# Hymba encoder layer on one core: the head projections of group A for two pairs of heads at a time, v and z_a with 512 weight columns a product

## The chip, the cores and the metric

One core of a Trainium2 chip runs the whole layer in one launch. The metric is the device time of an execution in microseconds. The kernel before took 1144.22 us (median of 3 runs, 1143.96 to 1146.23). Every array is float32 in memory; TensorE is fed with float32r, a shortened form of it.

## The reference, cut to what matters

The sequence has 256 tokens, the model 2048 channels, group A 16 heads of 128.

```python
hn   = rmsnorm(x, norm_w)
proj = hn @ w_in                       # 2048 x 18432: q, v, f_fwd, f_bwd, z_a, b, c, h, z_b
# group A, each head, both directions
f    = lb + (1 - lb) * sigmoid(f_logit);  k = 1 - f;  q = silu(q)
b    = cumsum(log f) in chunks of 64
o    = masked(q exp(b - b_mid) @ (k exp(b_mid - b)).T) @ v  +  (q exp(b)) @ state
o_a  = head_rmsnorm(o_fwd + o_bwd) * silu(z_a)
# group B
o_b  = rmsnorm(b * conv3(c * h)) * silu(z_b)
h    = x + concat(o_a, o_b) @ w_out
h    = h + (p @ w_ple) * sigmoid(h @ w_ple_gate)
out  = rmsnorm(h, final_norm_w)
```

## The kernel before

**Products in three parts.** A float32 operand is split into a high part that float32r holds exactly and a low part, the rest. ScalarE copies the high part (line 70), VectorE subtracts it (line 71). A product is then high x high + high x low + low x high, so each weight quarter of 1024 columns per partition costs one copy and one subtraction. `Stream` (lines 31 to 81) keeps a list of all weight blocks in the order of use, loads 1 MB at a time into three buffers (`raw`, on SyncE's queue) and splits quarters (`spl`, five buffers) three quarters ahead of their use. The activations `xs` are split once and stay.

**One block.** A block is 256 columns of `w_in` against all 2048 channels and 256 tokens, in 16 steps over the channels and two halves m. In each step and half there are two matmuls: one with 512 moving columns and one with 256 (lines 290 and 291). *Column-major* blocks (f_fwd, f_bwd, q and all of group B) hold the weights still and stream `xs` (high and low, 256 tokens each); *token-major* blocks (z_a and v) hold `xs` still and stream 256 weight columns, high and low. Each half of a block fills one PSUM buffer (`a`, four of them); `evac` adds its two halves with one ScalarE copy and one VectorE operation per m.

**Group A.** The loop runs over 8 pairs of heads. Each pair has the blocks f_fwd, f_bwd, q, z_a, v in this order, four weight quarters each. When z_a is done, `mix_pair` computes from f and q the forget gates, the cumulative sums (`tensor_tensor_scan` on VectorE), the exponentials, and on GpSimd the scaled copies kc, qc, kx. Two things then need TensorE for each head: `scores` (32-row products into `scps`, then the four `cx` products) and `outputs` (products of `s` and `sx` with `vt`). They are put among the blocks by `at(dt, fn)`: fn is issued when the counter of steps, which `tick()` raises once for each of the 16 steps of a block, is dt higher. For a pair the scores come 20 and 34 steps after `mix_pair`, the outputs 30 and 44; for the first pair all of them 16 steps later. `finish_pair`, called from the next pair's `mix_pair`, scales the outputs by their norm and sets `turn` 16 and 24 steps later: two transposes into the PSUM buffer `kv`, of which there is one, then ScalarE (line 368) and VectorE (line 369) write the two parts of `mixa`.

**The order on each engine** is made by a scheduler that places the recorded instructions by priority and dependence; the splits get a higher priority, so that they move ahead of the attention's work. On each engine instructions then run in the order that it left.

**First pair.** The first three blocks run together under a hand-written order while `x` and the weights arrive (lines 322 to 331). Their sums sit in the four `a` buffers and in `kv` and `tr`. The norms of the tokens (`rx`, `rbc`) follow from a second load of x.

Of the kernel before, what the change touches and what calls it, by code (L numbers as in the profile page):

```python
# [17 lines left out]
P = 128  # L18
D = 2048
T = 256  # L20
# [10 lines left out]
class Stream:  # L31
# [10 lines left out]
    def add(self, src):  # L42

        j = len(self.todo)
        _, k, n = src.shape
        self.todo.append((src, k, n))
        first = len(self.where)
        self.where += [(j, h) for h in range(k * n // 1024)]
        return list(range(first, len(self.where)))

    def load(self, j, k0=0, k1=None, pool=None):
        src, k, n = self.todo[j]
        if j not in self.raws:
            tag = f"raw{j}" if pool else "raw"
            self.raws[j] = (pool or self.rawp).tile([P, 2048], F32, tag=tag, name=f"raw{j}")
        dst = self.raws[j][:, : k * n].rearrange("p (k n) -> p k n", n=n)
        self.nc.sync.dma_start(dst[:, k0:k1], src[:, k0:k1])

    def open(self, i):
        j, h = self.where[i]  # L60
        n = self.todo[j][2]
        if j not in self.raws:
            self.load(j)
        half = self.raws[j][:, h * 1024 : (h + 1) * 1024].rearrange("p (k n) -> p k n", n=n)
        part = self.splp.tile([P, 2048], F32R, tag="spl", name=f"spl{i}")
        self.parts[i] = part.rearrange("p (k s n) -> p k s n", s=2, n=n)
        return half, self.parts[i]

    def split(self, r, v):
        self.nc.scalar.copy(out=v[:, :, 0, :], in_=r)  # L70
        self.nc.vector.tensor_tensor(out=v[:, :, 1, :], in0=r, in1=v[:, :, 0, :], op=ALU.subtract)  # L71
# [13 lines left out]
def tile_hymba_encoder(  # L85
# [193 lines left out]
    def gemm_part(acc, w, g, token_major, k0=0, k1=4):  # L279
        for k in range(k0, k1):  # L280
            kt = 4 * g + k
            for m in range(2):
                a = acc[m].rearrange("p a b -> p (a b)")
                if token_major:
                    lh, ll = xs[:, kt, 0, m * P : (m + 1) * P], xs[:, kt, 1, m * P : (m + 1) * P]
                    rf, rh = w[:, k, :, :].rearrange("p s n -> p (s n)"), w[:, k, 0, :]
                else:
                    lh, ll = w[:, k, 0, m * P : (m + 1) * P], w[:, k, 1, m * P : (m + 1) * P]
                    rf, rh = xs[:, kt, :, :].rearrange("p s n -> p (s n)"), xs[:, kt, 0, :]
                pe.matmul(a, lhsT=lh, rhs=rf, start=(kt == 0), stop=False)  # L290
                pe.matmul(a[:, :T], lhsT=ll, rhs=rh, start=False, stop=(kt == NKT - 1))  # L291
            tick()

    def gemm_in(c, i, token_major):
        acc = acc_in(c, i)
        for g in range(4):
            gemm_part(acc, ws.get(blocks[c, i][g]), g, token_major)
        return acc

    def evac(acc, dst, tmpp, token_major=False):  # L300

        for m in range(2):
            r = tmpp.tile([P, T], F32, tag="r", name="r", bufs=3)
            if token_major:
                act.activation(r, acc[m][:, 1, :], AF.Copy, scale=rx[:, m : m + 1])
                dve.scalar_tensor_tensor(
                    out=dst(m), in0=acc[m][:, 0, :], scalar=rx[:, m : m + 1], in1=r, op0=ALU.mult, op1=ALU.add
                )
            else:
                act.copy(out=r, in_=acc[m][:, 1, :])  # L310
                dve.tensor_tensor(out=dst(m), in0=acc[m][:, 0, :], in1=r, op=ALU.add)
# [10 lines left out]
    with tc.manual_schedule(engines={ENG.Activation, ENG.DVE, ENG.PE}):  # L322
        for g in range(4):
            parts = [ws.open(ids3[c][g]) for c in range(3)]
            for k0, k1 in PIECES[g]:
                for k in range(k0, k1):
                    x_split(4 * g + k)
                for half, v in parts:
                    ws.split(half[:, k0:k1], v[:, k0:k1])
                for c in range(3):  # L330
                    gemm_part(acc3[c], parts[c][1], g, False, k0, k1)
# [20 lines left out]
    def finish_pair(i, ogz, ss):  # L352

        rs = ap_.tile([P, 4], F32, tag="rs", name=f"rs{i}", bufs=2)
        act.activation(rs, ss, AF.Sqrt, bias=epst, scale=1.0 / P)
        dve.reciprocal(out=rs, in_=rs)
        for m in range(2):
            for h in range(2):
                dve.tensor_scalar(
                    ogz[:, m, h, :], ogz[:, m, h, :], rs[:, 2 * m + h : 2 * m + h + 1], None, op0=ALU.mult  # L360
                )

        def turn(h):
            hd = 2 * i + h
            tp = psm.tile([P, 512], F32, tag="kv", name=f"ogt{hd}")
            for m in range(2):
                pe.transpose(tp[:, m * P : (m + 1) * P], ogz[:, m, h, :], ident)
            act.activation(mixa[:, hd, 0, :], tp[:, :T], AF.Copy, scale=hgw[:, hd : hd + 1])
            dve.scalar_tensor_tensor(
                out=mixa[:, hd, 1, :], in0=tp[:, :T], scalar=hgw[:, hd : hd + 1],  # L370
                in1=mixa[:, hd, 0, :], op0=ALU.mult, op1=ALU.subtract,
            )

        for h in range(2):
            at(16 + 8 * h, lambda h=h: turn(h))

    last_pair = [None]

    def mix_pair(i, xf, qt, zt, vt):

# [4 lines left out]
        for n, t in (("q", qt), ("z", zt)):  # L385
            sg = ap_.tile([P, 2, T], F32, tag="sg", name=f"s{n}{i}")
            act.activation(sg, t, AF.Sigmoid)
            pool.tensor_tensor(out=t, in0=t, in1=sg, op=ALU.mult)
# [13 lines left out]
        if last_pair[0] is not None:  # L402
            last_pair[0]()
# [50 lines left out]
        ogz = ap_.tile([P, 2, 2, P], F32, tag="ogz", name=f"ogz{i}", bufs=2)  # L454
        ss = ap_.tile([P, 4], F32, tag="ss", name=f"ss{i}", bufs=2)
# [58 lines left out]
        def outputs(h):  # L514
            s, sx = st[h]
            o = psm.tile([P, 2, P], F32, tag="o", name=f"o{i}_{h}")
            hs = slice(h * P, (h + 1) * P)
# [4 lines left out]
            for m in range(2):  # L522
                act.activation(junk, o[:, m, :], AF.Square, accum_out=ss[:, 2 * m + h : 2 * m + h + 1])
            dve.tensor_tensor(out=ogz[:, :, h, :], in0=o, in1=zt[:, :, hs], op=ALU.mult)


        late = 16 if i == 0 else 0
        for h in range(2):
            at(late + 20 + 14 * h, lambda h=h: scores(h))
            at(late + 30 + 14 * h, lambda h=h: outputs(h))  # L530
        last_pair[0] = lambda: finish_pair(i, ogz, ss)

    for i in range(8):
        xf = ap_.tile([P, 2, 2, T], F32, tag="xf", name=f"xf{i}", bufs=2)
        evac(acc3[0] if i == 0 else gemm_in(B_FF, i, False), lambda m: xf[:, 0, m, :], ap_)
        evac(acc3[1] if i == 0 else gemm_in(B_FB, i, False), lambda m: xf[:, 1, m, :], ap_)
        qt = ap_.tile([P, 2, T], F32, tag="qt", name=f"qt{i}")
        evac(acc3[2] if i == 0 else gemm_in(B_Q, i, False), lambda m: qt[:, m, :], ap_)
        zt = ap_.tile([P, 2, T], F32, tag="zt", name=f"zt{i}")
        acc = gemm_in(B_ZA, i, True)  # L540
        if i == 0:
            xctx.close()
        evac(acc, lambda m: zt[:, m, :], ap_, True)
        vt = ap_.tile([P, 2, T], F32, tag="vt", name=f"vt{i}")
        mix_pair(i, xf, qt, zt, vt)
        evac(gemm_in(B_V, i, True), lambda m: vt[:, m, :], ap_, True)
# [10 lines left out]
    for i in range(8):  # L557
        cg = ctmp.tile([P, 2, T], F32, tag="cg", name=f"cg{i}", bufs=2)
        evac(gemm_in(B_CG, i, False), lambda m: cg[:, m, :], ctmp)
        hb = ctmp.tile([P, 2, T], F32, tag="hb", name=f"hb{i}", bufs=2)  # L560
        evac(gemm_in(B_HB, i, False), lambda m: hb[:, m, :], ctmp)
        if i == 0:
            last_pair[0]()
# [11 lines left out]
        evac(gemm_in(B_BG, i, False), lambda m: hb[:, m, :], ctmp)  # L575
        pool.tensor_tensor(out=cg, in0=cg, in1=hb, op=ALU.mult)
        y2 = ctmp.tile([P, 2, T], F32, tag="y2", name=f"y2_{i}")
        act.activation(y2, cg, AF.Square)
        pool.tensor_tensor(out=ysum, in0=ysum, in1=y2, op=ALU.add)
        evac(gemm_in(B_ZB, i, False), lambda m: hb[:, m, :], ctmp)  # L580
        by_norms(hb, rbc, 2)
        sz = ctmp.tile([P, 2, T], F32, tag="szb", name=f"szb{i}")
# [211 lines left out]
```

## Time and profile before

| | |
|---|---|
| runs | 1143.96, 1144.22, 1146.23 us |
| profiled execution | 1147.19 us, of it 1145.4 us from the first to the last instruction |
| mean granted clock of TensorE | 0.993 of full speed |
| TensorE, VectorE, ScalarE, GpSimd busy | 1129.6, 737.6, 644.5, 214.2 us |
| one pair of group A, from the third pair on | 60.54 us |
| weights and inputs read | 211.11 MB, 186 GB/s over the span |

A line of the profile names engine, line of the kernel before, operation, tiles and shape. TensorE's matmuls overlap each other, so the length of one is not its cost: the distance from one start to the next is. "Idle before" is the engine's own idle time, and what stands behind the arrow ended it. PEclk is the share of TensorE's clock that was granted in a stretch.

### The profile page before, as it was taken

To read this page: it belongs to the slowest core of one execution; us is meant where nothing else is said; L and a number is where in the kernel's file an instruction comes from. 1 tells how busy PE (TensorE), PEld (TensorE's weight loads), DVE (VectorE), ACT (ScalarE), POOL (GpSimd) and SP (SyncE) were. 2 spreads that over 40 slices of the span, in tenths; PEclk is the share of its full clock that TensorE was granted. 3 is DMA by queue.
4 is the path that set the end of the run, shared out by engine and by line. 5 is a ranking of instruction groups with operands and counts; after the bars stand their busy time and mean duration, and the time that the engine had idled before them with its cause. 6 is when DMAs were issued, how large, how long until landed. Compare 5 with 4: busy or idle time off the path is not lost.

```text
span 1145.4 us, 16984 instructions
## 1 busy us (share of the span) xinstructions
PE 1129.6 (99%) x6832; PEld 980.5 (86%) x6832; DVE 737.6 (64%) x957; ACT 644.5 (56%) x899; POOL 214.2 (19%) x167
## 2 busy tenths in 40 slices
PE   8999999999999999999999999999999999999997
PEld 7878888888888888888888888888888888888887
DVE  6785859585858686775566566556656555555664
ACT  6685767584858585765544444444545434434554
POOL 1032414140413223232121111211211000000011
PEclk9998999999999999999999999999999999999998
DMA  8753545455455545464555555555557555565542
GB/s 294 294 187 119 185 159 188 161 185 182 152 182 178 174 163 185 152 215 152 191 196 195 186 184 189 188 198 180 203 184 266 188 196 190 198 215 189 201 167 75
DMA packets 33487, 214.31 MB, mean 187 GB/s; under 512 B 3712, under 2 KB 5120, under 8 KB 9088
## 3 DMA queue, kind: packets, MB, share of 16 engines
q1 hardware_dynamic: 33264, 213.14, 54.1%
q8 instruction: 54, 0.88, 0.3%
q14 instruction: 25, 0.20, 0.1%
q10 hardware_dynamic: 144, 0.08, 0.0%
HBM read 211.11 MB, written 2.10 MB: 186 GB/s over the span
## 4 chain that ended last, share of the span: by engine, by line
PE 97%; DMA 1%; DVE 0%; POOL 0%; ACT 0%; SPq 0%; issue 0%; ACTq 0%; DVEq 0%
PE a L290 46%; PE a L291 23%; PE pg L640 3%; PE pg L639 3%; PE pg L641 3%; PE pa L639 3%; PE pa L641 3%; PE pb L641 3%; PE pb L639 3%; PE pa L640 3%; PE pb L640 3%; PE cx L509 1%; PE scps L467 1%; PE o L520 1%; PE o L519 1%; DMA xf<-in_xt_dram 1%
## 5 line engine op out<-in xcount | busy, mean ns | idle before, releaser
L71 DVE TENSOR_TENSOR spl<-raw,spl 128x1024 fp32r<-128x1024 f32 (+2 forms) x397 | 501.7, 1267 | 326.1 <-ACT spl L70 325.4
L290 PE MATMUL a<-xs,spl 128*128 128x512 f32 x1792 | 633.8, 398 | 2.8 <-DVE xs L237 1.8
L70 ACT CAST spl<-raw 128x1024 fp32r<-128x1024 f32 (+2 forms) x397 | 407.5, 1029 | 350.3 <-PE a L291 213.0
L291 PE MATMUL a<-xs,spl 128*128 128x256 f32 x1792 | 500.9, 280 | 0.2 <-DVE spl L71 0.2
L290 PEld LDWEIGHTS a<-xs,spl 128*128 128x128 f32 x1792 | 338.1, 189 | 79.7 <-ACT spl L70 2.2
L291 PEld LDWEIGHTS a<-xs,spl 128*128 128x128 f32 x1792 | 339.6, 190 | 0.8 <-DVE spl L71 0.5
L290 PE MATMUL a<-spl,xs 128*128 128x512 f32 x512 | 178.4, 392 | 0.0
L291 PE MATMUL a<-spl,xs 128*128 128x256 f32 x512 | 143.4, 280 | 0.0
L290 PEld LDWEIGHTS a<-spl,xs 128*128 128x128 f32 x512 | 95.8, 187 | 21.3
L291 PEld LDWEIGHTS a<-spl,xs 128*128 128x128 f32 x512 | 96.8, 189 | 0.0
L310 ACT COPY r<-a 128x256 f32<-128x256 f32 x112 | 40.9, 368 | 45.4 <-PE a L291 45.4
L698 POOL TENSOR_TENSOR hh<-hh,fw 128x512 f32<-128x512 f32 (+1 forms) x10 | 11.5, 1152 | 259.2 <-ACT gt L697 249.7
L639 PE MATMUL pg<-spl,ht 128*128 128x512 f32 (+1 forms) x160 | 55.6, 348 | 0.0
L641 PE MATMUL pg<-spl,ht 128*128 128x512 f32 (+1 forms) x160 | 55.5, 347 | 0.0
L640 PE MATMUL pg<-spl,ht 128*128 128x512 f32 (+1 forms) x160 | 55.5, 347 | 0.0
L639 PE MATMUL pa<-spl,mixa 128*128 128x512 f32 x128 | 50.4, 394 | 0.0
L641 PE MATMUL pa<-spl,mixa 128*128 128x512 f32 x128 | 49.9, 390 | 0.0
L640 PE MATMUL pa<-spl,mixa 128*128 128x512 f32 x128 | 49.9, 390 | 0.0
L639 PE MATMUL pb<-spl,mixb 128*128 128x512 f32 x128 | 49.8, 389 | 0.0
L640 PE MATMUL pb<-spl,mixb 128*128 128x512 f32 x128 | 49.8, 389 | 0.0
L641 PE MATMUL pb<-spl,mixb 128*128 128x512 f32 x128 | 49.8, 389 | 0.0
L505 POOL TENSOR_TENSOR s<-scm 128x256 f32<-128x256 f32 x16 | 18.0, 1123 | 102.3 <-DVE scm L503 102.3
(167 smaller groups left out, 1092.4 us busy)
## 6 DMA issues: line engine op xcount, KB each, us to landing
raw<-in_w_in_dram SPq DMA_DIRECT2D x138, 1024.0 KB, 5.0
raw<-in_w_out_dram SPq DMA_DIRECT2D x32, 1024.0 KB, 5.0
raw<-in_w_gate_dram SPq DMA_DIRECT2D x12, 1024.0 KB, 5.0
raw<-in_w_gate_end_dram SPq DMA_DIRECT2D x4, 1024.0 KB, 4.9
raw<-in_w_in_dram SPq DMA_DIRECT2D x6, 512.0 KB, 11.1
raw<-in_w_in_dram SPq DMA_DIRECT2D x9, 256.0 KB, 6.4
xf<-in_xtok_dram SPq DMA_DIRECT2D x2, 1024.0 KB, 12.6
hh<-in_xtok_dram SPq DMA_DIRECT2D x1, 2048.0 KB, 8.2
```

Source lines behind the costliest of these rows:

```text
L70: self.nc.scalar.copy(out=v[:, :, 0, :], in_=r)
L71: self.nc.vector.tensor_tensor(out=v[:, :, 1, :], in0=r, in1=v[:, :, 0, :], op=ALU.subtract)
L290: pe.matmul(a, lhsT=lh, rhs=rf, start=(kt == 0), stop=False)
L291: pe.matmul(a[:, :T], lhsT=ll, rhs=rh, start=False, stop=(kt == NKT - 1))
L310: act.copy(out=r, in_=acc[m][:, 1, :])
L467: pe.matmul(scps[s0 : s0 + Q, 2 * d + hf, t0 : t0 + w], lhsT=lhsT, rhs=rhs, start=True, stop=True)
L505: pool.tensor_tensor(out=s, in0=sm[:, 0:2, :], in1=sm[:, 2:4, :], op=ALU.add)
L509: pe.matmul(cx[:, d, :], lhsT=kx[:, d, h, :], rhs=qc[:, d, h, :], start=True, stop=True)
L639: pe.matmul(acc[m], lhsT=lh, rhs=w[:, k, 0, :], start=(kt == 0), stop=False)
L640: pe.matmul(acc[m], lhsT=lh, rhs=w[:, k, 1, :], start=False, stop=False)
L641: pe.matmul(acc[m], lhsT=ll, rhs=w[:, k, 0, :], start=False, stop=(kt == nk - 1))
L698: pool.tensor_tensor(out=h, in0=h, in1=fw[:, cs], op=ALU.mult)
```

## The change

Group A goes by two pairs of heads (i and i + 1, four times). For both pairs the three column-major blocks f_fwd, f_bwd, q run first, six in a row. Then v of both pairs runs as one product of 512 weight columns (`gemm_two`), then z_a of both in the same way. In `gemm_two` a step and half has three matmuls of 512 columns (high x high, high x low, low x high) in place of two times 512 + 256, and `tick()` is called for each half, 32 times a product. A weight load for it is two transfers of 512 KB, one from each pair's block, side by side in one `raw` buffer. Its sum is taken out of PSUM by one ScalarE operation per m, with no VectorE operation.

`mix_pair` is cut in two: `mix_forgets` (norms, sigmoids, logarithms, forget gates) right behind each pair's q, and the rest, for the first pair at once and for the second 16 steps into v. z_a's gate (`gate_two`) and the scaling by the norm (`finish_two`) follow when both pairs' outputs exist, while the next two pairs' blocks run; the gate is now multiplied in there and `outputs` only copies. Counted in steps from the end of the six blocks, the scores stand at 9, 15, 46 and 52, the outputs at 38, 42, 55 and 61; for the first two pairs the scores are 18 and 12 steps later and the second pair's outputs 12. The four turns of two pairs are issued 48, 50, 52 and 54 steps after the next two pairs' first q block. The scratch `r` has two buffers instead of three, and in group B `y2` and `szb` share one.

```diff
     def load(self, j, k0=0, k1=None, pool=None):
-        src, k, n = self.todo[j]
+        srcs, k, n = self.todo[j]
...
+        for b, src in enumerate(srcs):
+            self.nc.sync.dma_start(dst[:, b, k0:k1], src[:, k0:k1])
...
-    for i in range(8):
-        for c in (B_FF, B_FB, B_Q, B_ZA, B_V):
-            blocks[c, i] = sum((ws.add(w_in[c + i, h]) for h in range(2)), [])
+    for i in range(0, 8, 2):
+        for ii in (i, i + 1):
+            for c in (B_FF, B_FB, B_Q):
+                blocks[c, ii] = sum((ws.add(w_in[c + ii, h]) for h in range(2)), [])
+        for c in (B_V, B_ZA):
+            blocks[c, i] = sum(
+                (ws.add(*(w_in[c + i + b, q // 2, :, 4 * (q % 2) : 4 * (q % 2) + 4] for b in range(2))) for q in range(4)), []
+            )
...
+    def gemm_two(c, i, dst):
+        acc = [psg.tile([P, 512], F32, tag="g", name=f"a{c}_{i}_{m}") for m in range(2)]
+        for kt in range(NKT):
+            w = ws.get(blocks[c, i][kt // 2])
+            for m in range(2):
+                lh, ll = xs[:, kt, 0, m * P : (m + 1) * P], xs[:, kt, 1, m * P : (m + 1) * P]
+                pe.matmul(acc[m], lhsT=lh, rhs=w[:, kt % 2, 0, :], start=(kt == 0), stop=False)
+                pe.matmul(acc[m], lhsT=lh, rhs=w[:, kt % 2, 1, :], start=False, stop=False)
+                pe.matmul(acc[m], lhsT=ll, rhs=w[:, kt % 2, 0, :], start=False, stop=(kt == NKT - 1))
+                tick()
+        for m in range(2):
+            act.activation(dst[:, m, :], acc[m], AF.Copy, scale=rx[:, m : m + 1])
...
-            dve.tensor_tensor(out=ogz[:, :, h, :], in0=o, in1=zt[:, :, hs], op=ALU.mult)
+            dve.tensor_copy(ogz[:, :, h, :], o)
...
-        late = 16 if i == 0 else 0
-        for h in range(2):
-            at(late + 20 + 14 * h, lambda h=h: scores(h))
-            at(late + 30 + 14 * h, lambda h=h: outputs(h))
+        late = 18 if i == 0 else 0
+        at(late + 9, lambda: steps[0][0](0))
+        at(late + 15, lambda: steps[0][0](1))
+        at(late + 16, lambda: steps.append(mix_pair(i + 1, *forgets[1])))
+        late = 12 if i == 0 else 0
+        at(38, lambda: out(0, 0))
+        at(42, lambda: out(0, 1))
+        at(late + 46, lambda: steps[1][0](0))
+        at(late + 52, lambda: steps[1][0](1))
+        at(late + 55, lambda: out(1, 0))
+        at(late + 61, lambda: out(1, 1))
+        gemm_two(B_V, i, vt)
+        gemm_two(B_ZA, i, zt)
+        def rest():
+            gate_two(i, zt)
+            at(30 if i < 6 else 6, lambda: finish_two(i, ogs, ss, zt))
+            for hd in range(4):
+                at((48 if i < 6 else 20) + 2 * hd, lambda hd=hd: turn(2 * i + hd, ogs[hd // 2]))
+        last_two[0] = rest
```

The order changes at three places that matter below. The first is VectorE some 78 us into the program, around the end of the fourth to sixth block. Before, the two operations on `vt0` free the PSUM buffers of the first pair's v; they stand behind the split of quarter 27:

```order
L71 TENSOR_TENSOR spl27_856<-raw13_827,spl27_856 128x4x256
L430 TENSOR_TENSOR gx_153<-dd0_645,pf0_644 128x2x3
L431 TENSOR_TENSOR gx_153<-pf0_644,lf0_635 128x2x3
L306 SCALAR_TENSOR_TENSOR vt0_625<-a8_0_0_677,few_79,r_759 128x256
L432 TENSOR_TENSOR gx_153<-gx_153,dd0_645 128x2x3
L306 SCALAR_TENSOR_TENSOR vt0_625<-a8_0_1_678,few_79,r_762 128x256
L438 TENSOR_TENSOR pf0_644<-qt0_477,pf0_644 128x512
L311 TENSOR_TENSOR xf1_765<-a16_1_0_766,r_848 128x256
```

In the changed kernel the buffers that the next product waits for there are those of the second pair's f_bwd (`a24_1`), and their two operations on `xf1` stand ahead of the split of quarter 26:

```order
L451 TENSOR_TENSOR gx_153<-dd0_634,pf0_633 128x2x3
L452 TENSOR_TENSOR gx_153<-pf0_633,lf0_624 128x2x3
L328 TENSOR_TENSOR xf1_487<-a24_1_0_674,r_756 128x256
L453 TENSOR_TENSOR gx_153<-gx_153,dd0_634 128x2x3
L328 TENSOR_TENSOR xf1_487<-a24_1_1_675,r_759 128x256
L77 TENSOR_TENSOR spl26_827<-raw13_824,spl26_827 128x2x512
L458 TENSOR_TENSOR dd0_634<-xf0_467,dd0_634 128x512
L459 TENSOR_TENSOR pf0_633<-qt0_468,pf0_633 128x512 x2
```

So the operations that free the PSUM buffers stand two splits nearer to the start. The second place is VectorE at the first pair's outputs, where the copy into `ogz0` frees the single PSUM buffer `o` for the second head's output. Before:

```order
L503 COPY_PREDICATED scm0_149<-tri_143,scps_155 128x512
L71 TENSOR_TENSOR spl30_945<-raw15_943,spl30_945 128x4x256
L71 TENSOR_TENSOR spl31_982<-raw15_943,spl31_982 128x4x256
L524 TENSOR_TENSOR ogz0_675<-o0_0_956,zt0_484 128x2x128
L311 TENSOR_TENSOR xf1_765<-a24_1_0_854,r_973 128x256
```

In the changed kernel (pf1 and dd1 are the second pair's cumulative sums, from `mix_pair(i + 1)`):

```order
L432 SCALAR_TENSOR_TENSOR pf1_1071<-smask_140,lf1_858 128x256
L436 SCALAR_TENSOR_TENSOR pf1_1071<-lf1_858,smask_140 128x256
L442 TENSOR_TENSOR dd1_1072<-pf1_1071 128x256
L445 TENSOR_TENSOR dd1_1072<-pf1_1071 128x256
L442 TENSOR_TENSOR dd1_1072<-pf1_1071 128x256
L77 TENSOR_TENSOR spl37_1136<-raw18_1108,spl37_1136 128x2x512
L445 TENSOR_TENSOR dd1_1072<-pf1_1071 128x256
L451 TENSOR_TENSOR gx_153<-dd1_1072,pf1_1071 128x2x3
L452 TENSOR_TENSOR gx_153<-pf1_1071,lf1_858 128x2x3
L453 TENSOR_TENSOR gx_153<-gx_153,dd1_1072 128x2x3
L544 COPY ogz0_1120<-o0_0_1121 128x2x128
```

The copy out of `o` now stands behind the second pair's scans. The third place is ScalarE at the turns of a steady pair. Before, one turn is among splits and copies:

```order
L70 CAST spl65_2008<-raw32_1982 128x4x256
L511 COPY sx2_0_1980<-cx2_0_1977 128x256
L70 CAST spl66_2029<-raw33_2027 128x4x256
L368 ACTIVATE mixa_460<-ogt3_2003,vec_81 128x256
L70 CAST spl67_2065<-raw33_2027 128x4x256
```

In the changed kernel (the second to fourth of four turns):

```order
L375 ACT_TABLE_LOAD
L375 ACTIVATE sq3_1926<-qt3_1641 128x512
L417 ACTIVATE mixa_460<-ogt1_1949,vec_81 128x256
L76 CAST spl70_2034<-raw35_2031 128x2x512
L417 ACTIVATE mixa_460<-ogt2_1960,vec_81 128x256
L530 COPY sx2_0_2020<-cx2_0_2017 128x256
L417 ACTIVATE mixa_460<-ogt3_1977,vec_81 128x256
L76 CAST spl71_2108<-raw35_2031 128x2x512
```

The four turns now follow each other with one or two instructions between, among the second pair's forget gates. On TensorE 12 matmuls of 512 columns stand between the first turn and the second, 15 and half of the scores between the second and third, and the other half of the scores, `cx` and 4 matmuls between the third and fourth.

More of the change, by code (lines that the diff above doesn't have):

```diff
@@ L330, in tile_hymba_encoder @@
                 for c in range(3):
[L331 removed]
+                    gemm_part(acc3[c], parts[c][1], g, k0, k1)
     rctx.close()
@@ L350, in c64, with mix_forgets @@
         return t.rearrange("p h (c t) -> p h c t", t=CH)
[L352 to L357, printed above, removed]
-            for h in range(2):
[L359 to L379, printed above, removed]
+    def mix_forgets(i, xf, qt):
         by_norms(xf.rearrange("p a b t -> p (a b) t"), rbc, 4)
@@ L522, in outputs @@
             for m in range(2):
[L523 to L540 removed]
+                act.activation(junk, o[:, m, :], AF.Square, accum_out=ss[:, m, h : h + 1])
@@ L549, in tile_hymba_encoder @@
+        last_two[0] = rest
+    for i in range(0, 8, 2):
+        two_pairs(i)
+    last_two[0]()
     mixb = None
```

141 lines of the change are left out of this document (90 added, 51 removed).

## The prediction

> **What bounds the kernel now.** I read the page first, its busy times and the chain that ended last.
>
> ```profile
> span 1145.4 us, 16984 instructions
> PE 1129.6 (99%) x6832; PEld 980.5 (86%) x6832; DVE 737.6 (64%) x957; ACT 644.5 (56%) x899; POOL 214.2 (19%) x167
> PE 97%; DMA 1%; DVE 0%; POOL 0%; ACT 0%; SPq 0%; issue 0%; ACTq 0%; DVEq 0%
> ```
>
> TensorE sets the end: 97% of the chain is matmuls following each other. So only three things can pay: fewer or shorter matmuls, less waiting of TensorE, or a higher clock. Whatever VectorE and ScalarE save is worth nothing unless TensorE was waiting for it. Next I read the waits of TensorE alone, those after the start:
>
> ```profile
> PE scps L467 <- POOL qc L446: 1.7, 1, 1.7
> PE a L290 <- DVE gx L432: 0.9, 1, 0.9
> PE scps L467 <- POOL kc L446: 0.8, 1, 0.8
> PE cx L509 <- POOL kx L452: 0.8, 1, 0.8
> ```
>
> Each occurs once, so they belong to one place, 4.2 us together. The busy times by stretch show where (the columns are the stretch, its length, the five engines' busy time, PEclk, DMA share, GB/s):
>
> ```profile
> 78.00:90.00 12.00, 7.76 (x75) 6.24 (x74) 9.21 (x15) 6.17 (x11) 6.96 (x6) 0.92 0.42 138
> 90.00:103.00 13.00, 13.00 (x103) 11.24 (x103) 5.48 (x7) 5.33 (x12) 0.55 (x1) 0.82 0.33 120
> 138.35:198.89 60.54, 60.54 (x432) 53.34 (x436) 43.86 (x61) 40.96 (x61) 16.55 (x11) 1.00 0.51 171
> 259.43:319.97 60.54, 60.54 (x432) 53.33 (x436) 44.07 (x61) 40.98 (x61) 16.56 (x11) 1.00 0.51 175
> ...
> 79.00:80.00 1.00, 0.54 (x3) 0.53 (x4) 0.78 (x3) 0.99 (x2) 0.00 (x0) 1.00 0.68 90
> 88.00:89.00 1.00, 0.32 (x1) 0.32 (x2) 0.72 (x1) 0.00 (x0) 0.83 (x2) 0.50 0.84 164
> 94.00:95.00 1.00, 1.00 (x5) 0.90 (x4) 0.16 (x1) 0.00 (x0) 0.00 (x0) 0.60 0.00 0
> 95.00:96.00 1.00, 1.00 (x7) 0.87 (x7) 0.00 (x0) 0.00 (x0) 0.00 (x0) 1.00 0.00 0
> ```
>
> A steady pair is 60.54 us in which TensorE never rests, while VectorE has 44 and ScalarE 41 us of work: no stall is left to remove there. In the 12 us from 78 on TensorE works only 7.76. These are the first pair's scores, whose kc, qc and kx come from GpSimd too late. Behind the idle time comes a second loss: from 88 to about 95 us the clock is half.
>
> **Term 1, fewer matmuls.** What a matmul costs is the distance of starts. I take a column-major stretch of group B (13 pairs of 512 + 256) and the output projection, whose three 512-column products have the form of the new ones:
>
> ```profile
> 600.33 0.39 PE L290 MATMUL a<-xs,spl 128*128 128x512 f32 x1
> ...
> 604.83 0.40 PE L290 MATMUL a<-xs,spl 128*128 128x512 f32 x1
> ...
> 919.96 0.39 PE L639 MATMUL pa<-spl,mixa 128*128 128x512 f32 x1
> ...
> 925.40 0.39 PE L639 MATMUL pa<-spl,mixa 128*128 128x512 f32 x1
> ```
>
> 4.50 us / 13 = 0.3462 us for 768 columns; 5.44 / 24 = 0.2267 us for 512. The old form needs two pairs, 0.6923 us, for what three new matmuls do in 0.6800: 12.3 ns less. There are 32 of these in each product, two products and four passes, 256 in all: **3.15 us**. The columns are the same, 1536 on both sides, so all of it is a fixed cost of a matmul, of which there are 256 fewer. Sum by the two rows: fixed part f = 12.3 ns, for 768 columns = 2f + 768c and 512 = f + 512c.
>
> The Trainium skill, in "TensorE: Matmul & The Clock Gate", section "Wait — 56ns, not 53.3ns?", states a fixed cost of only about 2.5 ns per matmul at full clock. By it term 1 would be 0.64 us; the rows here show five times that, for this float32r form with a weight load ahead of every matmul, so I keep 3.15.
>
> **Term 2, the stall at the first pair.** The scores of pair 0 move from 36 steps behind `mix_pair` to 27 steps into v, behind two whole blocks: `mix` is issued in step 15 of f_fwd(1), the scores 48 + 27 − 15 = 60 steps later. The first 33 of these are column-major steps of 0.69 us, the last 27 take 0.68, so 41 us, where before 36 x 0.69 = 25 us missed by 3.3. The chain ahead has the same work plus the second pair's `by_norms` (one GpSimd operation and a sigmoid), so 1.7 + 0.8 + 0.8 = 3.3 us go.
>
> The 0.9 us have another cause, PSUM. The next block needs the buffers of v(0), which VectorE emptied late:
>
> ```profile
> 77.55 1.21 DVE L71 TENSOR_TENSOR spl<-raw,spl 128x1024 fp32r<-128x1024 f32 x1
> ...
> 78.84 0.47 DVE L306 SCALAR_TENSOR_TENSOR vt<-a,few,r 128x256 f32<-128x256 f32 x1
> ...
> 79.31 0.47 DVE L306 SCALAR_TENSOR_TENSOR vt<-a,few,r 128x256 f32<-128x256 f32 x1
> ...
> 79.46 0.47 PE L290 MATMUL a<-xs,spl 128*128 128x512 f32 x1 [0.90 <-DVE gx L432]
> ```
>
> The same buffer rule holds for the changed kernel (v(0) needs f_bwd(1)'s), but the order has two splits fewer ahead, 2 x 1.2 = 2.4 us, more than 0.9. So it goes too: **4.2 us** for both. If it does not, 0.9 come back.
>
> **Term 3, the clock.** PEclk 0.92 over 12 us and 0.82 over 13 are 0.96 + 2.34 = 3.3 us of clock; half of the 0.68 us in which TensorE was idle from 88 to 89 comes off: **2.9 us**. In the steady pairs, and from 79 to 80 in the middle of the lone 0.9 us wait, PEclk is 1.00, so single waits of that size do not cost clock.
>
> **Term 4, new waits.** The pieces, by groups of instructions:
>
> ```profile
> L71 DVE TENSOR_TENSOR spl<-raw,spl 128x1024 fp32r<-128x1024 f32 (+2 forms) x397 | 501.7, 1267 | 326.1 <-ACT spl L70 325.4
> L70 ACT CAST spl<-raw 128x1024 fp32r<-128x1024 f32 (+2 forms) x397 | 407.5, 1029 | 350.3 <-PE a L291 213.0 <-PE pb L641 53.1 <-PE pa L641 41.5
> L310 ACT COPY r<-a 128x256 f32<-128x256 f32 x112 | 40.9, 368 | 45.4 <-PE a L291 45.4
> L387 ACT ACT_TABLE_LOAD x15 | 19.2, 1283 | 12.3 <-DVE zt L306 12.1
> L411 DVE TENSOR_TENSOR_SCAN pf<-smask,lf 128x256 f32<-128x256 f32 x16 | 17.2, 1074 | 0.0
> L503 DVE COPY_PREDICATED scm<-tri,scps 128x512 f32<-128x512 uint32 x16 | 11.8, 739 | 2.3 <-PE scps L467 2.3
> L415 DVE TENSOR_TENSOR_SCAN pf<-lf,smask 128x256 f32<-128x256 f32 x16 | 10.8, 673 | 0.0
> L369 DVE SCALAR_TENSOR_TENSOR mixa<-ogt,vec,mixa 128x256 fp32r<-128x256 f32 x16 | 7.6, 475 | 0.0
> L368 ACT ACTIVATE mixa<-ogt,vec 128x256 fp32r<-128x256 f32 x16 | 7.5, 470 | 0.0
> L524 DVE TENSOR_TENSOR ogz<-o,zt 128x256 f32<-128x256 f32 x16 | 6.7, 421 | 6.7 <-ACT jk L523 6.7
> L421 DVE TENSOR_TENSOR dd<-pf 128x256 f32<-128x256 f32 x16 | 6.7, 419 | 0.3
> ```
>
> *The first pair's second output* (once). It needs the buffer `o`, freed by the copy into `ogz0`. Ahead of that on VectorE stand, from the end of the scores: the mask 0.74, four scans 2 x 1.07 + 2 x 0.67 = 3.49, four subtractions 1.68, one split 1.27, the copy 0.42, about 7.6, plus half of a split that is under way, 0.6: 8.2 us. TensorE has meanwhile 9 steps x 0.68 = 6.1, the `cx` products 0.64 and the first output, which I count like `cx`: 7.4. Wait 0.8; ends 0 and 2.1 (a whole split more). I take **0.7**. In later passes the scores are 23 steps ahead of the outputs and it is covered.
>
> ```profile
> 138.35 0.70 PE scps L467 x31
> 139.05 0.64 PE cx L509 x4
> ```
>
> *The turns* (three passes among v, a fourth in group B). `kv` is one buffer: the second turn waits until ScalarE and VectorE have read the first. Behind the first turn stand a copy of q's sum 0.37, a split's copy 1.03, on VectorE its subtraction 1.27, and line 369's 0.48: 3.15 us against 12 x 0.2267 = 2.72 on TensorE, 0.4 of waiting. The second turn has a table load 1.28, a sigmoid and a split ahead against 15 matmuls, 3.4 us, and some 0.15 of scores; the third mask and split against scores and `cx`, 0.7 + 0.64, and 4 matmuls, 0.9. Both come out near zero. The lower end is 0 (the scheduler placed the matmuls between for this), the upper one table load more, 0.4 + 1.28 = 1.7 per pass. I take 0.5, nearest to the one chain that I can add up: **1.5 us** for three, 0 to 5.1. Behind a waiting turn queue v's matmuls alone; their splits are three quarters ahead.
>
> **Edits at nothing.** Per two pairs VectorE loses eight operations of line 306 and ScalarE gets 4 longer ones for 8; the gates only move. Both stay under the 44 and 41 of 60.5 us above, so TensorE covers them, and if it did not they would show as waits for `spl`. The 64 transfers of 512 KB replace 32:
>
> ```profile
> raw<-in_w_in_dram SPq DMA_DIRECT2D x138, 1024.0 KB, 5.0
> ```
>
> 1 MB lands in 5.0 us and is used up in two quarters per 2.7 us, three buffers deep; SyncE's queue carries nothing else then. An issue more per MB, even if its landing took half as long again, stays hidden behind the two buffers ahead.
>
> **Sum.** 3.15 + 4.2 + 2.9 − 0.7 − 1.5 = 8.05 us. On the profiled execution's own 1147.19 us (1145.4 and 1.8 around it) this is 1139.1. The median shown is 2.97 lower, just about term 3: these runs may have kept the clock. If so, 1144.22 − 5.15 = 1139.1; if not, 1136.2. I say **1138**.
>
> **Rivals.**
> - *Turns become the bound, slower.* If a table load, a split's copy and its subtraction stand ahead of each later turn (1.28 + 1.03 + 1.27, with the turn's own 0.47 + 0.48 in all 4.5 us against 2.7), each waits 1.8, a pass 5.4, and as at 88 us the clock drops for 2.9 more. Three passes of 8.3 less the 10.25 gained: 1144.2 + 25 − 10 = 1159; the waits decide from 10.25 / 3 = 3.4 us per pass on. For it: ScalarE's order. Against: 0.4 for the only chain that I can close. 10%.
> - *The first stall stays.* v(0) waits for f_bwd(1)'s buffers and the scores for GpSimd after all, since VectorE worked 9.2 of the 12 us from 78 on. Terms 2 and 3 fall out: 1144.2 − 3.15 + 2.2 = 1143.3. Against: 16 us more slack. 12%.
> - *No new wait.* 1144.2 − 10.25 = 1134. 18%.
> - *Term 1 is not there*: with `xs` held still and splits read through two strides, three products take the 0.6923 us of the old two pairs; 1138 + 3.15 = 1141.2. Against: the output projection's rows. 4%. By the skill's 2.5 ns a matmul, above, it would be 1140.5.
>
> **Chances.** Forecast 56%. A measurement of this kernel tells about 0.2%, 2.3 us, from no change: below 1141.9 is faster. Forecast (53 of its 56), no new wait and most of the fourth give 0.74; the stay of the stall and the forecast's rest 0.16; slower 0.10. The range runs from all gains without a wait, 1133.5, to 1145, the stall's stay with the turns' upper end.
>
> **What would show it.** Right: three 512-column matmuls in v and z_a 0.227 apart; no wait of `scps` or `cx` for GpSimd; PEclk 1.00 from 20 us on; a wait of at most 2 us at the first pair's second `o`, and three of about 0.5 at `ogt`; two pairs in 120.3 + 0.5. Wrong: waits for `spl` in v or z_a, waits of DMA, several microseconds at `ogt`, a half clock in the steady passes.

## The result, and the profile after

The changed kernel takes 1158.77 us (median; 1151.66 to 1159.80), the kernel before beside it 1145.22. The ratio is 1.0105 with a 95% interval of 1.0064 to 1.0146: slower by about 1%, where 1138 was forecast. In a second set of runs it was 1157.11 against 1144.93, ratio 1.0104 (1.0075 to 1.0133). Its times do not scatter around the median. Of the eleven executions on record four lie at 1151.7 to 1154.1 and seven at 1158.4 to 1161.6, nothing between. The first profile is of a run of the lower group, with 1151.66 us. From its page, the busy times and the chain that ended last:

```profile
span 1149.8 us, 16467 instructions
PE 1130.6 (98%) x6576; PEld 968.5 (84%) x6576; DVE 725.6 (63%) x921; ACT 636.4 (55%) x874; POOL 219.1 (19%) x167
PE 85%; DVE 5%; ACT 4%; POOL 4%; DMA 2%; issue 1%; SPq 0%; ACTq 0%; DVEq 0%; POOLq 0%
```

The 256 fewer matmuls are there (6832 before), but PE's busy time has not fallen (1129.6 before), and the chain that ended last now runs through VectorE and ScalarE for 9%. The waits of TensorE, the largest line only, and the busy times of the stretches that stalled before:

```profile
PE ogt L416 <- DVE mixa L418: 8.0, 4, 2.7
```

```profile
78.00:90.00 12.00, 12.00 (x54) 9.94 (x53) 9.85 (x12) 11.89 (x16) 7.65 (x6) 1.00 0.53 176
90.00:103.00 13.00, 13.00 (x135) 10.58 (x134) 9.24 (x11) 8.14 (x11) 1.43 (x2) 1.00 0.72 243
...
207.60:334.10 126.50, 123.88 (x803) 104.57 (x794) 84.47 (x112) 80.42 (x117) 34.82 (x22) 0.99 0.51 172
...
328.00:331.40 3.40, 3.40 (x10) 2.63 (x9) 2.65 (x2) 2.03 (x3) 2.59 (x2) 0.50 0.53 175
454.30:457.70 3.40, 3.40 (x9) 2.67 (x8) 2.76 (x3) 2.14 (x3) 2.66 (x2) 0.51 0.42 166
```

The first pair's stall is gone, and the clock is whole there. In its place stand 8.0 us of waits at the turns: about 2.5 us at the second turn in each of three passes, and 0.4 at the last group of turns, in group B. Two pairs now take 126.5 us, where before they took 2 x 60.54 = 121.1, and behind the wait the clock is half for 3.4 us.

Why the turn waits is read from the order of time on ScalarE (first fence), VectorE (second) and TensorE (third) around the first turn of the third pass, which TensorE ends at 321.95. A row has its start, its duration, engine, line and operation.

```profile
320.64 1.28 ACT L382 ACT_TABLE_LOAD   x1
321.93 0.60 ACT L382 ACTIVATE lf<-xf,lb,oml 128x256 f32<-128x256 f32 x1
322.44 1.04 ACT L76 CAST spl<-raw 128x1024 fp32r<-128x1024 f32 x1
323.38 1.09 ACT L382 ACTIVATE lf<-xf,lb,oml 128x256 f32<-128x256 f32 x2
324.37 0.35 ACT L327 COPY r<-a 128x256 f32<-128x256 f32 x1
324.62 1.04 ACT L76 CAST spl<-raw 128x1024 fp32r<-128x1024 f32 x1
325.57 0.47 ACT L417 ACTIVATE mixa<-ogt,vec 128x256 fp32r<-128x256 f32 x1
```

```profile
325.70 1.23 DVE L77 TENSOR_TENSOR spl<-raw,spl 128x1024 fp32r<-128x1024 f32 x1
326.84 0.48 DVE L418 SCALAR_TENSOR_TENSOR mixa<-ogt,vec,mixa 128x256 fp32r<-128x256 f32 x1
```

```profile
327.38 0.44 PE L416 MATMUL ogt<-ident,ogz 128*128 128x128 f32 x2 [2.45 <-DVE mixa L418]
```

The turn falls just where the sixth block ends. There `mix_forgets` of the second pair puts its logarithms on ScalarE: three of them, two split copies and a copy of a sum stand ahead of the turn's own copy, 3.6 us, and then a split on VectorE. From the turn to the free buffer it takes 5.4 us against 2.7 of matmuls; I had added 3.15.

### The profile page after: what moved, and what is told of

Same layout as the page of the kernel before. It is cut to its first block, busy times and chain, and to the rows that moved or that the text cites. A ratio compares the mean times of both kernels' runs of the same rounds, so it can differ in the third digit from the quotient of the medians.

```text
span 1149.8 us, 16467 instructions
## 1 busy us (share of the span) xinstructions
PE 1130.6 (98%) x6576; PEld 968.5 (84%) x6576; DVE 725.6 (63%) x921; ACT 636.4 (55%) x874; POOL 219.1 (19%) x167
## 4 chain that ended last, share of the span: by engine, by line
PE 85%; DVE 5%; ACT 4%; POOL 4%; DMA 2%; issue 1%; SPq 0%; ACTq 0%; DVEq 0%; POOLq 0%
PE a L298 28%; PE a L299 15%; PE a L317 5%; PE a L318 5%; PE a L316 5%; PE pg L704 3%; PE pg L703 3%; PE pg L705 3%; PE pa L703 3%; PE pa L705 3%; PE pa L704 3%; PE pb L703 3%; PE pb L705 3%; PE pb L704 3%; DVE spl L77 2%; POOL qc L467 2%
## 5 line engine op out<-in xcount | busy, mean ns | idle before, releaser
L298 PE MATMUL a<-xs,spl 128*128 128x512 f32 x1792 | 628.1, 395 | 1.3 <-DVE xs L249 0.9
L76 ACT CAST spl<-raw 128x1024 fp32r<-128x1024 f32 (+2 forms) x397 | 408.4, 1030 | 346.9 <-PE a L299 168.6
L298 PEld LDWEIGHTS a<-xs,spl 128*128 128x128 f32 x1792 | 336.2, 188 | 79.3 <-issue 1.4
L316 PE MATMUL a<-spl,xs 128*128 128x512 f32 x256 | 103.8, 406 | 0.0
L317 PE MATMUL a<-spl,xs 128*128 128x512 f32 x256 | 101.5, 396 | 0.0
L318 PE MATMUL a<-spl,xs 128*128 128x512 f32 x256 | 101.2, 395 | 0.0
L318 PEld LDWEIGHTS a<-spl,xs 128*128 128x128 f32 x256 | 48.9, 191 | 10.3
L316 PEld LDWEIGHTS a<-spl,xs 128*128 128x128 f32 x256 | 49.1, 192 | 9.2
L317 PEld LDWEIGHTS a<-spl,xs 128*128 128x128 f32 x256 | 48.9, 191 | 9.0
L703 PE MATMUL pb<-spl,mixb 128*128 128x512 f32 x128 | 49.8, 389 | 0.0
L704 PE MATMUL pb<-spl,mixb 128*128 128x512 f32 x128 | 49.8, 389 | 0.0
```

The source lines that it names most:

```text
L76: self.nc.scalar.copy(out=v[:, :, 0], in_=r)
L316: pe.matmul(acc[m], lhsT=lh, rhs=w[:, kt % 2, 0, :], start=(kt == 0), stop=False)
L317: pe.matmul(acc[m], lhsT=lh, rhs=w[:, kt % 2, 1, :], start=False, stop=False)
L318: pe.matmul(acc[m], lhsT=ll, rhs=w[:, kt % 2, 0, :], start=False, stop=(kt == NKT - 1))
L703: pe.matmul(acc[m], lhsT=lh, rhs=w[:, k, 0, :], start=(kt == 0), stop=False)
L704: pe.matmul(acc[m], lhsT=lh, rhs=w[:, k, 1, :], start=False, stop=False)
```

## The experiments

**The changed kernel again.** No edit.

> The changed kernel once more, nothing edited. The changed kernel's runs lie at 1151.7 and at 1158.4 to 1159.8, with the same granted clock, 7 us apart. Pace theory: the column-major pair (512 + 256 columns) has two paces, 0.347 and 0.353 us, and keeps the one that it is in until something else runs on TensorE; a run of 1158 to 1160 then shows 0.353 in the 32 blocks of group B (1024 pairs x 0.0065 = 6.7 us), a run near 1152 shows 0.347 there as the first profile did. Rival, a stall: the 7 us are waits of TensorE somewhere (weights, or the turns), the pace in group B is 0.347 in every run, and the waits of a run of 1159 add up to about 7 us more than in the first profile. Either way the median is 1158 to 1160 and the waits ahead of the turns are 8 us.

The profile is of a run of 1160.15 us. Its waits at the turns are the same, 7.9 us. What differs is the pace of group B. The stretch from 600 to 800 us, column-major matmuls alone, in the run of 1151.66 (first) and in this one:

```profile
600.00:800.00 200.00, 200.00 (x1156) 176.34 (x1155) 121.43 (x147) 95.61 (x123) 36.15 (x28) 1.00 0.56 190
```

```profile
600.00:800.00 200.00, 200.00 (x1134) 173.48 (x1133) 118.29 (x147) 94.38 (x121) 35.79 (x27) 1.00 0.54 185
```

1156 matmuls against 1134 in the same 200 us, both without a pause and at full clock: 0.346 us a pair against 0.353. Over the 1024 pairs of group B this is 6.9 us, about the distance of the two groups. (The run of 1160.15 has three half-clock windows and the first one two, which is 1.7 us more: 8.6 together, and the runs differ by 8.5.) The stall rival falls.

**The turns spread.**

```diff
-            at(30 if i < 6 else 6, lambda: finish_two(i, ogs, ss, zt))
+            at(20 if i < 6 else 6, lambda: finish_two(i, ogs, ss, zt))
...
-                at((48 if i < 6 else 20) + 2 * hd, ...)
+                at((28 if i < 6 else 20) + 5 * hd, ...)
```

> The four turns of a pass are spread five steps apart inside the fifth and sixth column-major block (at 28, 33, 38 and 43 steps, in place of 48, 50, 52 and 54), and the rows are finished at 20 in place of 30. Turn theory: the second turn of each pass waits because the first turn's two evacuations queue on ScalarE and VectorE behind the second pair's logarithms and splits; spread, the 8.0 us of waits and the two half-clock windows that follow them (3.4 us each, half of that lost) go, so 11 us less than the unchanged changed kernel, about 1148, or 1141 in a run with the fast pace in group B. Pace theory adds that the turns, which now interrupt the blocks, may bring the pair's pace in passes two and three from 0.353 to 0.347, up to 3 us more. Rival, the waits only move (to the splits, or to the scores that follow): within 2 us of the unchanged one.

1143.91 us (1142.42 to 1145.45), ratio 0.9991 (0.9982 to 1.0): 13 us below the unedited one. The waits at the turns fell from 8.0 to 3.5 us, no half clock is left between the start and the end, and group B ran at 0.347. Less went than I expected from the waits, more from the pace of group B: all eleven runs lie in one group.

**Two banks.**

```diff
-        tp = psm.tile([P, 512], F32, tag="kv", name=f"ogt{hd}")
+        tp = psm.tile([P, 512], F32, tag=("kv", "tr")[hd % 2], name=f"ogt{hd}")
```

> The turns stay where they are, but take turns in two PSUM banks, the carried products' bank beside their own. Turn theory: the second turn no longer waits for the first one's evacuation, the third does for 1 us at most, so 6 to 8 us of waits go and with them most of the half clock: 8 to 11 us less than the unchanged one, the same as with the turns spread if no pace is touched. Rival: the wait passes to the third turn or to the carried product of the scores that follows in that bank; then 3 us or less are won.

The waits of TensorE, and the third turn of the third pass in the order of time:

```profile
PE ogt L416 <- DVE mixa L418: 7.0, 3, 2.4
```

```profile
329.04 0.44 PE L416 MATMUL ogt<-ident,ogz 128*128 128x128 f32 x2 [2.42 <-DVE mixa L418]
```

1151.68 us: the waits are 7.0 instead of 8.0, now at the third turn, and the three half-clock windows are there. As the rival had it, the wait only moved. So a second buffer alone does not help, because the first turn's way through ScalarE and VectorE is what is late. The 5 us to the median of the unedited kernel are group B, at 0.347 in this profile.

**Spread, and two banks.** Both edits.

> Both edits of the two runs before: the turns spread five steps apart and taking turns in two PSUM banks. Spread alone left 1.2 us of wait at the second turn of three passes (3.5 us), because the first turn's evacuation still stands behind a block's evacuations and splits on ScalarE and VectorE; two banks alone only passed the wait on to the third turn, two steps later. Together the bank of a turn is asked for ten steps (14 us) after the one before it was filled: no wait ahead of a turn is left, 3.5 us less than spread alone, 1140.4. Rival, the pace: with other interruptions the column-major pairs may come out of a turn at 0.353 in place of 0.347, and group B with them (6.7 us): then 1144 to 1147 without any wait, and a pace of 0.353 in the trace says so.

1138.68 us (1138.24 to 1139.13), ratio 0.9940 (0.9923 to 0.9958). All waits of TensorE that are left lie in the first 26 us:

```profile
PE wps L179 <- DVE wz L174: 1.1, 1, 1.1
PE a L299 <- DVE spl L77: 1.0, 2, 0.8
PE a L298 <- ACT spl L76: 0.6, 1, 0.6
```

It is 1.7 less than I expected. Of the two traces the one with the turns only spread waited 2.4 us for the first splits of weights (`PE a L298 <- ACT spl L76`), this one 0.6; whether the medians differ by that is not shown. This is the forecast's time, by a kernel whose only difference is where the turns stand and what they write to. It beats both kernels.

**The first pair's scores early.** On that kernel, the first part of the change undone:

```diff
-        at(late + 9, lambda: steps[0][0](0))
-        at(late + 15, lambda: steps[0][0](1))
+        at(9, lambda: steps[0][0](0))
+        at(15, lambda: steps[0][0](1))
```

> Turns spread and in two banks; the first pair's two score steps 18 steps earlier (9 and 15 steps into its row-major block in place of 27 and 33), as the later passes have them: about 82.6 us in place of 94.9. This undoes the part of the change that gave the first pair's operands time. In the trace of the kernel without this edit GpSimd ends the last scaled keys for the scores at 84.2 and those for the carried product at 85.3. First-stall theory (the stalls of the kernel before at 84.3, 86.7 and 87.9 came from GpSimd's and VectorE's chain, and the half clock from the stalls): waits of 1.6 us ahead of the scores and some 0.5 ahead of the carried product return, and one or two half-clock windows of 3.4 us behind them (1.7 us each): 4 to 5.5 us more than 1138.7, so 1143 to 1144. Rival, that the first stall was worth little and the gain of the spread turns came from the fewer products alone: 1139 to 1140.5, no half clock.

```profile
PE cx L528 <- ACT sx L530: 1.1, 1, 1.1
...
PE scps L486 <- POOL kc L467: 0.9, 1, 0.9
PE cx L528 <- POOL kx L473: 0.8, 1, 0.8
```

1141.99 us: 3.3 more, of which 2.7 are the three waits. GpSimd's `kc` and `kx` are late again, as in the kernel before; the largest wait, 1.1, is for ScalarE's copy `sx`. The clock stayed whole, so by the medians I had expected 1 to 2 us too much. The two kernels were measured in different sets of runs, though: by the ratios to the kernel before (0.9979 and 0.9940) the difference is 4.5 us, so the price lies between 3.3 and 4.5.

**What sets the pace.** Seven runs put a small unused matmul of zeros into the stream, with n moving columns (its price, from the starts around it, is 0.23 to 0.24 us):

```diff
+        if <block>:
+            nudge = psm.tile([P, 512], F32, tag="o", ...)
+            pe.matmul(nudge[:, :n], lhsT=wz, rhs=wz[:, :n], start=True, stop=True)
         acc = acc_in(c, i)
```

*Ahead of all 32 blocks of group B, n = 128, in the changed kernel:*

> Ahead of each of the 32 column-major blocks of group B stands one small matmul of zeros (128x128, float32, into a bank that nothing else uses there); it computes nothing that is used. All else is the changed kernel. Its own price is about 0.3 us each, 10 us in all at most. Pace theory: it interrupts the stream, so group B does not stay at 0.353 for all 32 blocks: the runs no longer lie 7 us apart as a whole, blocks change between 0.347 and 0.353, and the median without the small matmuls' own time is 2 to 7 us below the unchanged one. Stall theory: the runs keep two groups 7 us apart, and the time is that of the unchanged one plus the matmuls' own.

1159.84 us (1158.90 to 1160.81), one group; group B at 0.347. A block with its small matmul takes 11.33 us in place of 32 x 0.3467 = 11.09. The small matmuls cost 32 x 0.24 = 7.7, so without them 1152.1, the lower group in each of four runs.

*Widths, on the kernel with the turns mended:*

> The same kernel with one small unused matmul of zeros ahead of each of the 18 column-major blocks of passes two to four, its moving side 16, 32, 64, 96, 112 or 128 columns wide in a changing order. It asks what sets the pace: if the length of the interruption does, each width leads to the same pace every time (three trials of each), and a width that always leads to 0.347 is the one to use; if the state before does, or chance, the widths show both. Its price is some 18 x 0.2 = 3.6 us; if half of the 15 blocks that ran at 0.353 (0.2 us each) come to 0.347, 1.5 us come back: 1142.5 against 1140.4 for the kernel without them.

1140.67 us, 2.0 more than without, for 18 x 0.23 = 4.1 of small matmuls. The pace of the pairs behind each, read from the starts (where 16 columns led to 0.353 the pairs ahead had run at 0.347; two of the 0.347 behind 32 and 128 came from 0.353):

```
columns  between pairs, after a stream of pairs    between v/z_a and the pairs
16       0.353, 0.353                              0.353
32       0.347, 0.347                              (outputs follow at once)
64       0.347, 0.347
96       0.347, 0.347                              0.353
112      0.347, 0.353
128      0.347, 0.347
```

Behind the sixth block's small matmul of each pass (112, 64, 128 columns) a turn follows after two pairs, too soon to read a pace.

*One ahead of the first block of passes two to four, 32 and then 16 columns:*

> Turns spread and in two banks, and one small unused matmul of zeros with 32 moving columns at the start of the six column-major blocks of passes two, three and four (three in all). Pace theory: without it these blocks run at 0.353 from their start to the first turn in each pass; in the run with widths 32 columns led to 0.347 three times of three. If the interruption's length sets the pace, 132 + 151 + 151 pairs come from 0.353 to 0.347, 2.8 us less, and the small matmuls cost 0.1 each: 1136.2 against 1138.7 without them. Rival, that the pace depends on chance or on the state before: 1137 to 1139, with blocks of both paces.

> The same with 16 columns in place of 32. In the run with widths 16 columns led to 0.353 three times of three. Pace set by the length: the blocks of passes two to four start at 0.353 as they did without the small matmul, 1138.7 + 3 x 0.1 = 1139. Rival, any small matmul at this place does it: 1136.2, as with 32 columns.

1139.46 and 1139.98 us. With both widths passes three and four begin at 0.353, so between v/z_a and the pairs the small matmul changes nothing: a miss for the theory that its length alone decides. In pass two, where two outputs follow soon, the long stretch behind them ran at 0.347 with both widths, 16 included, and at 0.353 without the small matmul.

*One ahead of the second block instead, 32 columns:*

> Turns spread and in two banks; the small unused matmul of zeros with 32 moving columns ahead of the second column-major block of passes two to four, inside the stream of pairs, in place of ahead of the first, where it stood between the 512-column products and the pairs and changed nothing. If 32 columns inside a stream of pairs lead from 0.353 to 0.347 (in the run with widths and in the changed kernel's group B they did), 118 pairs in each of two or three passes gain 0.0065 each, 0.8 us a pass, less 0.1 for the small matmul: 1136.4 to 1137.3. If what leads there is not the width: 1138.7 to 1139.5, blocks at 0.353 behind it.

A stretch of the third pass in the kernel without (first) and with it:

```profile
262.00:302.00 40.00, 40.00 (x228) 34.67 (x228) 29.22 (x42) 28.77 (x36) 8.41 (x5) 1.00 0.51 170
```

```profile
265.00:305.00 40.00, 40.00 (x233) 35.28 (x232) 30.07 (x43) 28.67 (x36) 8.76 (x6) 1.00 0.52 180
```

In all three passes the pairs went from 0.353 to 0.347. The time, 1138.31 us (ratio 0.9942, 0.9928 to 0.9955), cannot be told from 1138.68: three passes gain 3 x 118 x 0.0067 = 2.4 us, and 0.7 for the small matmuls and three new waits of 0.5 for a block's buffers take most of it back.

*In the changed kernel with its turns as they were, one ahead of the third block of group B, 32 and then 16 columns:*

> The changed kernel unedited but for one small unused matmul of zeros with 32 moving columns ahead of the third column-major block of group B, behind the last turn. The unedited runs lie in two groups, 1151.7 to 1154.1 and 1158.4 to 1161.6. Pace theory: 31 of 32 blocks, no: the 30 blocks that follow always run at 0.347, all runs lie at 1152 to 1154. Rival (the pace plays no part, or the small matmul does not set it): two groups as before, median 1157 to 1159.

> The same with 16 columns. Pace theory, with the length of the interruption as what sets it: the 30 blocks always run at 0.353, all runs lie at 1158 to 1161. Rival (any interruption does, or none): 1152 to 1154 throughout, or two groups as in the unedited kernel.

1154.46 us (1152.55 to 1158.63, two of six above 1157.8) and 1161.26 (1160.05 to 1162.11, all four in the upper group). The stretch of group B with 32 columns (first) and with 16:

```profile
600.00:800.00 200.00, 200.00 (x1155) 176.65 (x1154) 121.75 (x148) 95.65 (x123) 35.89 (x27) 1.00 0.55 190
```

```profile
600.00:800.00 200.00, 200.00 (x1135) 173.55 (x1134) 118.97 (x146) 94.22 (x121) 35.77 (x27) 1.00 0.54 186
```

Two kernels that differ in 16 columns of one idle matmul are 6.8 us apart. So the pace of group B is what parts the traced runs of the two groups, and an interruption inside the stream sets it: there the pace behind 16 columns was 0.353 3 times of 3, behind 32 and 128 it was 0.347 in every profile. With 32 two runs still came out long; I have no trace of those.

## Why the prediction was wrong, step by step

**The step that failed is term 4, the turns.** I put 0.5 us a pass, 0 to 1.7, and measured 2.4 to 2.7. The chain that I closed held one copy and one split ahead of the turn; the second pair's logarithms, which `mix_forgets` issues at that very place, were not in it. I had named ScalarE's order as the case for "Turns become the bound" and given it 10%, because I weighed it only for the later turns. That rival names the right kind of loss, at the first turn and not at the later ones, and smaller: 2.5 us of waits and mostly 1.7 of clock a pass, 4.2 together, where it had 5.4 and 2.9. That it hit the time, 1159, is luck: what its sum had too much, group B's pace added, of which it knew nothing.

**The clock, as a follow-up of the turns.** In six traces that keep the turns where the change put them, 16 of 18 of these waits are followed by a half-clock window of 3.4 us, which costs 1.7. I had no term for this outside the rival. The Trainium skill ("TensorE: Matmul & The Clock Gate", section "What's actually happening") says that the window is free-running, 3413 ns; the two windows shown above start at 328.0 and 454.3 us, 37 x 3.413 = 126.3 apart, and agree. Its section "Why this matters for your kernels" asks for no idle gaps over about 3 us; here gaps of 2.2 to 2.7 us were enough, and those of 0.8 to 1.2 were not.

Why two of the 18 waits cost no clock shows when TensorE's busy time is read window by window. In the first profile the stretches of one clock between the first change and the last are 320.85, 3.41, 122.88, 3.41 and 686.08 us long, all multiples of 3.413, so the borders of the windows can be counted from the half one at 327.96. There the second pass's wait of 2.67 us lies across a border, 1.77 us in one window and 0.90 in the next, and PEclk stays at 1.00 (first three rows). The third pass's 2.45 us lie in one window, and the next one is half (last two):

```profile
198.25:201.67 3.42, 1.65 (x8) 1.03 (x6) 2.97 (x5) 3.42 (x8) 0.00 (x0) 1.00 0.15 31
201.67:205.08 3.41, 2.51 (x12) 2.12 (x13) 3.41 (x5) 3.27 (x5) 1.41 (x2) 1.00 0.78 281
205.08:208.50 3.42, 3.42 (x55) 2.62 (x54) 2.40 (x5) 1.90 (x4) 1.48 (x1) 1.00 0.53 140
...
324.55:327.96 3.41, 0.96 (x6) 0.53 (x5) 3.41 (x9) 3.39 (x7) 0.23 (x1) 1.00 0.58 142
327.96:331.37 3.41, 3.41 (x10) 2.64 (x9) 2.69 (x3) 2.07 (x3) 2.63 (x2) 0.50 0.54 178
```

The other exception, in the kernel with 128 columns ahead of every block, splits into 0.99 and 1.43. In all fourteen traces, without the first and last 8 us, every window at whole clock in which TensorE waited 1.89 us or more is followed by a half one, 20 of them, and none in which it waited 1.77 or less.

**What no step contained: two paces of the same stream.** The pair of 512 + 256 columns runs at 0.347 or 0.353 us. My rows came from group B of the kernel before, at 0.347, and I took them for the form's cost. In the changed kernel, and in all kernels made from it, the pairs of passes three and four and of group B's first block, which follow v and z_a without other work between, begin at 0.353 in every trace; in the passes they stay so to the next wait or turn, about five blocks later, and run at either pace behind it. In the traced run of the upper group the rest of group B runs there too, and by their times so it does in seven of the eleven. The kernel before interrupts its blocks every few microseconds and keeps the fast pace from the second pair on, but for 18 pairs in each.

*Term 1* was right as to the form, and the pass still gained nothing. Starts of every third matmul in v of the changed kernel:

```profile
214.59 0.39 PE L316 MATMUL a<-spl,xs 128*128 128x512 f32 x1
...
221.39 0.39 PE L316 MATMUL a<-spl,xs 128*128 128x512 f32 x1
```

6.80 / 30 = 0.2267 us, as forecast. The fixed cost of a matmul that I worked out is less firm than I took it for: 2 x (0.3467 − 1.5 x 0.2267) is 13 ns at the fast pace of the pairs, and 27 with 0.3533 in place of 0.3467. And the pass did not become shorter. With every wait gone, two passes' first carried products stand 121.4 us apart, against 121.1 before and 120.3 predicted:

```profile
326.34 0.71 PE L528 MATMUL cx<-qc,kx 128*128 128x128 f32 x4
...
447.75 0.71 PE L528 MATMUL cx<-qc,kx 128*128 128x128 f32 x4
```

Of the 192 pairs of a pass 168 run at 0.353 there, where two pairs of heads had 36 before: 132 x 0.0067 = 0.9 us, and 120.3 + 0.9 = 121.2. Added up from start to start, the column-major pairs take 68.2 us a pass in both kernels. v and z_a take 44.7 against 44.4 before, where 192 x 0.2267 are 43.5. Most of the 1.2 on top lies at the starts just before the scores and just behind the carried products and the outputs (0.31 to 0.32 us in place of 0.2267); before, these stood among the pairs. So what term 1 earns in an undisturbed stream, 0.8 a pass, is given back, by the slower pace and at the starts around the scores and outputs.

*Term 2* was right: no `scps` or `cx` waits for GpSimd, v(0)'s buffers cost nothing, and put back early the scores cost 3.3 to 4.5 us. *Term 3* was right as to the place, PEclk is 1.00 from 78 to 103 us. How much of it the median runs of before had lost stayed as unclear as I left it; the three waits of 0.8 to 1.1 us in the kernel with early scores cost no clock.

*The first pair's second output*, 0.7 in term 4: no wait there, the lower end. *The edits at nothing*: right; no wait for a transfer and none for a split in v or z_a.

Sum with what was measured, for the kernel with the turns mended: the profiled execution of before, 1147.19, less 4.2 and 2.9 for the first pair, less 1.7 for a half clock of 3.4 us at the start of before that the mended kernel's trace does not have, is 1138.4; the mended kernel's profiled execution took 1138.48. The 0.3 by which each pass grew (121.4 against 121.1) is not in this sum, so a fit to 0.1 is in part luck. For the changed kernel itself 8.0 of waits and 2 x 1.7 of clock come on top, 1149.9 against 1151.66, and in most runs 6.9 for group B, 1156.8 against the medians of 1157.1 and 1158.8. One to two microseconds stay without a name.

## What to carry to other kernels

Before an evacuation is costed, read what the order puts on its engine at that very moment, from the other steps that the change sets at the same block's end: a chain of 3 us became one of 5 behind three logarithms. A second buffer helps only when the chain also has the time; spread and buffered together the wait was gone, spread alone left 3.5 of 8.0 us, two banks alone 7.0. And a duration taken from a stretch of the kernel before is the price of that stretch: look whether the same form runs at another pace elsewhere in the same trace before it is carried into a new order.

## What the runs showed of the hardware that I had not expected

A stream of alternating 512- and 256-column matmuls, each with its own weight load, has two paces at full clock and without any wait, 0.347 and 0.353 us a pair. It keeps the one it is in for up to 960 pairs, and a matmul of some 0.2 us between can change it: inside the stream 16 moving columns led to the slower, 32, 64, 96 or 128 to the faster, 112 once to each. Between 512-column matmuls and the pairs none of the widths tried (16, 32, 96, 128) led to the faster one. What in the engine keeps the pace, and why two of six runs with 32 columns came out long, is open.

The clock fell to half by windows of 3.41 us, and a wait counted by how much of it lay in one window. Behind a window at whole clock with 1.89 us or more of waits came a half one in all 20 cases, behind 1.77 or less in none, so a wait of 2.67 us across a border cost no clock.
